# A 512-column matmul for the high and low activations of a dense expert loop, with one subtraction moved to GpSimd

## The chip, the cores and the metric

One core of one Trainium2 chip runs the whole kernel. The metric is device time in microseconds (us); the number to predict is the median over runs of the changed kernel.

## The reference

The kernel computes one decoder layer for 512 tokens of width 1024: a mixing sub-layer (sparse attention beside a gated linear recurrence), a layer norm, a PEER sub-layer with 16384 single-neuron experts, and a second layer norm. Only the PEER part is touched:

```python
q = (xb @ w_q).reshape(PEER_BLOCK, PEER_HEADS, 2, PEER_KEY_DIM // 2)
s = jnp.einsum('thpd,hpkd->thpk', q, sub_keys).astype(jnp.float32)
...
g = jax.nn.softmax(best, axis=-1).astype(xb.dtype)
h = jax.nn.gelu(jnp.einsum('td,thkd->thk', xb, u[experts]))
return jnp.einsum('thk,thkd->td', g * h, v[experts])
```

Every token picks 128 experts (8 heads of 16). Its output is the sum over them of g * gelu(x.u) * v.

## The kernel before

The tokens stand in four blocks of 128. Blocks 0 and 1 take the **row path**: for each of the 128 experts of a token, GpSimd issues a gather of a row of `u` or `v` for the 128 tokens (`gather`, L627), and VectorE works it off with one instruction over 1024 columns (`gu` at L651, which also sums; `hsA<-gv` at L664). The gathered rows stand in a ring of GB = 4 buffers. `pump(n)` puts n such rows at a place of the program.

Blocks 2 and 3 take the **dense path** (`dense`): their 256 tokens meet all 16384 experts, 128 experts in each of 128 steps j. The sparse expert weights are first scattered into a matrix G. Then, in each step:

- `into_hidden(j, n, hp)`, n = 0 and 1: half of the transposed rows of `u` (128x512) is loaded and split by `split` into a high part in fp32r (ScalarE, L760) and the low remainder (VectorE, L762). TensorE sums three products into `hp`: u high times h low (`hTl`), u high times h high (`hTh`), u low times h high. The u part is the stationary operand, h is streamed in 256 columns (L771): 24 matmuls in a step.
- `weigh(j, hp)`: ScalarE takes the gelu of `hp` into `w` (L776), VectorE multiplies by G (L777), ScalarE makes the high part `wh` (L779), VectorE the low part `wl` (L781).
- `out_of_hidden(j, n, wh, wl)`: half of the rows of `v` is loaded and split likewise, and for each of two token blocks three products are summed into `acc` (L791): 12 matmuls of 512 columns in a step. The weights used here are those of one step earlier.

The rings of the loop: 4 buffers for `u`, 3 for `v`, 6 for the split parts, 2 each for `hp`, `wh` and `wl`, one for `w`. The rest of the rows of blocks 0 and 1 is spread over the steps by `pump`. The order of the instructions on each engine is not that of the program text: a scheduler sets it when the kernel is built, and each engine then works its own list strictly in order. SyncE (SP) issues the loads of `u` and `v`.

Of the kernel before, what the change touches and what calls it, by code (L numbers as in the profile page):

```python
# [24 lines left out]
DENSE = (2, 3)  # L25
# buffers of the rings of tiles
HGB = 5
# [6 lines left out]
PJ = 16  # L34
# rows of experts worked off at each such place of the program (sel: one at every second step)
PUMP = {"cw": 4, "qi": 4, "hf": 4, "hq": 4, "hi": 4, "hg": 3, "qa": 2, "hgrn": 1, "att": 4, "mix": 1, "sel": 2,
        "q0": 7, "q1": 0, "q2": 0, "q3": 0}
# rows of block 0's sum that the tensor engine takes: after the queries, and beside the dense weights
PEK1 = 14
PEK2 = 38  # L40
PEPRE = 8
PEG = 60
# tokens of each four whose weights ScalarE multiplies in
GACTS = (3, 4)
# a row of experts at every so manyth group of the dense weights
GPUMP = 3
# the dense step by which all rows are worked off
DLAST = 127
# [3 lines left out]
def tile_decoder_layer(ctx, tc, a, out):  # L52
# [70 lines left out]
    def layer_norm(ys, os_, g, b, nm):  # L123
        """Each y is a tile or a list of its parts along the features."""
        n = len(ys)
        mv = cst.tile([128, n, 2], F32, name="mv" + nm, tag="ln_mv", bufs=2)
        parts = [y if isinstance(y, list) else [y[:, k * 512:(k + 1) * 512] for k in range(2)] for y in ys]
        for i in range(n):
            st = cst.tile([128, 2, 6], F32, name=f"st{nm}_{i}", tag="ln_st", bufs=2)
            for k in range(2):  # L130
                nc.vector.bn_stats(st[:, k, :], parts[i][k])  # L131
            nc.vector.bn_aggr(mv[:, i, :], st)
        ve = cst.tile([128, n], F32, name="ve" + nm, tag="ln_ve", bufs=2)
        nc.vector.tensor_scalar(ve, mv[:, :, 1], EPS, None, op0=ALU.add)
        r = rsqrt(ve, n, nm)
        for i, o in enumerate(os_):
            if isinstance(ys[i], list):
                for k in range(2):
                    sl = slice(k * 512, k * 512 + 512)
                    nc.vector.scalar_tensor_tensor(o[:, sl], parts[i][k], mv[:, i, 0:1], g[:, sl],  # L140
                                                   op0=ALU.subtract, op1=ALU.mult)
            else:
                nc.vector.scalar_tensor_tensor(o, ys[i], mv[:, i, 0:1], g, op0=ALU.subtract, op1=ALU.mult)  # L143
            nc.vector.scalar_tensor_tensor(o, o, r[:, i:i + 1], b, op0=ALU.mult, op1=ALU.add)  # L144
# [24 lines left out]
    hsA = cst.tile([128, 2, 1024], F32, name="hsA")  # L169
    hsB = cst.tile([128, 2, 1024], F32, name="hsB", tag="hsB")  # L170
    hTh = cst.tile([128, 8, 256], F32R, name="hTh")
    hs = [hsA[:, 0, :], hsA[:, 1, :], hsB[:, 0, :], hsB[:, 1, :]]
# [6 lines left out]
    def tok_major(blocks, xT, w, name):  # L179
        """x W for each block, tokens on partitions."""  # L180
        ps_ = [bank(f"{name}{b}") for b in blocks]
# [11 lines left out]
    def feat_major(blocks, xT, w, name):  # L193
        """(x W)^T for all blocks at once, features on partitions: a bank for each 128 features."""
        m = w.shape[-1] // 128
# [22 lines left out]
    def lower_bound():  # L218
# [6 lines left out]

        # lower bound of the forget gate: f = fa + fc * tanh(z / 2)
        fa = pre.tile([128, 512], F32, name="fa")
# [41 lines left out]
    def hgrn(b, pr, mixT):  # L269
# [35 lines left out]
        for par in range(2):  # L305
            ap_ = bank(f"at{b}_{par}", "hg")
            for j in range(4):
# [3 lines left out]
                                    tri[:, None, :].to_broadcast([128, 4, 128]), op=ALU.mult)  # L311
        # the states before each chunk of 32
        S = []
# [86 lines left out]
    def select(b, pr):  # L400
        """What to add to the negated attention scores of the keys that the index doesn't choose."""
        nk = (b + 1) * 128
# [90 lines left out]
    def queries(blocks, hT):  # L493
        """Sub-key scores and, for each of the 16 lists, its 16 best."""
        nt = 128 * len(blocks)
# [53 lines left out]
    def best16(b, g, sv, si, bv, pos):  # L549
        # a pair (a, b) can be among the 16 best only if (a + 1) * (b + 1) <= 16; the places keep the pairs' order  # L550
        s4 = sv[:, g * 4:g * 4 + 4, :].rearrange("p (h z) k -> p h z k", z=2)
# [15 lines left out]
    def routing(b, half, sv, si, bv, pos):  # L567
        """The experts and their weights for four of the block's heads."""
        H = slice(half * 4, half * 4 + 4)
        C = slice(half * 64, half * 64 + 64)  # L570
        # place -> the two ranks
        p2 = pos[:, H, :].rearrange("p h k -> p (h k)")
# [20 lines left out]
        nc.vector.tensor_copy(rbb, t1)  # L593
        # rank -> sub-key
        si4 = si.rearrange("p (h z) k -> p h z k", z=2)
# [18 lines left out]
        if b not in DENSE:  # L614
            nc.vector.scalar_tensor_tensor(idx[b][half], val[1], 128.0, val[0], op0=ALU.mult, op1=ALU.add)
        # softmax over the 16 kept, whose first is their maximum
        g3 = gate[:, b, C].rearrange("p (h k) -> p h k", h=4)
# [27 lines left out]
    def peer_gather(b):  # L645
        """Yields True after each row of experts is worked off, False where it waits for pe_gather."""
        hd = cst.tile([128, 128], F32, name=f"hd{b}", tag="hd")
# [24 lines left out]
    def pe_gather(n, p):  # L672
        """A part of block 0's sum over the rows of v on the tensor engine: diag(weight) @ rows; yields after each."""
        while 0 not in weighted:
# [27 lines left out]
    def dense(den, dps):  # L702
        """Tokens of the DENSE blocks against every expert, with the experts' weights scattered to a dense matrix."""
        nb = len(DENSE)
        T = 128 * nb
        tr = {}
        hTl = consts_loaded["hTl"]
        for i, b in enumerate(DENSE):
# [56 lines left out]
        def into_hidden(j, n, hp):  # L765
            u = den.tile([128, 512], F32, name=f"u{j}_{n}", tag="u", bufs=UB)
            nc.sync.dma_start(u.rearrange("p (k i) -> p k i", k=4), a["ut"][j, :, n * 4:n * 4 + 4, :])
            uh, ul = split(f"u{j}_{n}", u)
            for q, (ut, ht) in enumerate(((uh, hTl), (uh, hTh), (ul, hTh))):
                for k in range(4):  # L770
                    nc.tensor.matmul(hp, ut[:, k * 128:(k + 1) * 128], ht[:, n * 4 + k, :],  # L771
                                     start=(n + q + k == 0), stop=(n == 1 and q == 2 and k == 3))

        def weigh(j, hp):
            w = den.tile([128, T], F32, name=f"w{j}", tag="w")
            nc.scalar.activation(w, hp, AF.Gelu_apprx_tanh)  # L776
            nc.vector.tensor_tensor(w, w, G[:, j, :], op=ALU.mult)  # L777
            wh = den.tile([128, T], F32R, name=f"wh{j}", tag="wh", bufs=2)
            nc.scalar.copy(wh, w)  # L779
            wl = den.tile([128, T], F32R, name=f"wl{j}", tag="wl", bufs=2)  # L780
            nc.vector.tensor_tensor(wl, w, wh.bitcast(F32), op=ALU.subtract)  # L781
            return wh, wl

        def out_of_hidden(j, n, wh, wl):
# [3 lines left out]
            for i in range(nb):  # L788
                sl = slice(i * 128, (i + 1) * 128)
                for q, (wt, vt) in enumerate(((wl, vh), (wh, vh), (wh, vl))):  # L790
                    nc.tensor.matmul(acc[i][n], wt[:, sl], vt, start=(j == 0 and q == 0), stop=(j == 127 and q == 2))  # L791

        def residual():
            ia = gat.tile([128, 128], F32, name="ia", tag="dg", bufs=1)
            nc.scalar.mul(ia, ident, ALPHA)
            for i in range(nb):
                for n in range(2):
                    for c in range(4):
                        for t in (hTl, hTh):
                            nc.tensor.matmul(acc[i][n][:, c * 128:(c + 1) * 128],  # L800
                                             t.bitcast(F32)[:, n * 4 + c, i * 128:(i + 1) * 128], ia,
                                             start=False, stop=False)
# [4 lines left out]
        for j in range(129):  # L807
            if j < 128:
                hp = dps.tile([128, 512], F32, name=f"hp{j}", tag="hp", bufs=2)[:, :T]
                into_hidden(j, 0, hp)  # L810
            want = total * min(j + 1, DLAST) // DLAST
            pump(want - due)
# [5 lines left out]
            if j == DLAST:  # L818
                gb = ln2_consts(1)
                finish(1, gb)  # L820
            if j < 128:
                into_hidden(j, 1, hp)
                ws_new = weigh(j, hp)
            if j:
# [7 lines left out]
    def stage(blocks, xT):  # L832
# [31 lines left out]
        if blocks != [0]:  # L864
            hTl = cst.tile([128, 8, 256], F32R, name="hTl", tag="hsB")
            consts_loaded["hTl"] = hTl
            for k in range(0, 8, 2):
                x = hT[:, k:k + 2, 128:384]
                nc.scalar.copy(hTh[:, k:k + 2, :], x)
                nc.vector.tensor_tensor(hTl[:, k:k + 2, :], x, hTh[:, k:k + 2, :].bitcast(F32), op=ALU.subtract)  # L870
            for _ in pe_gather(PEK1, [bank(f"pv{i}", "hg") for i in range(2)]):
# [57 lines left out]
```

## Time and profile before

| what | value |
|---|---|
| runs | 1651.08, 1656.95, 1659.08 us; median 1656.95 |
| span of the profiled execution, first to last instruction | 1647.0 us |
| TensorE matmul busy | 1456.9 us (88%), 7858 matmuls |
| VectorE busy | 1387.7 us (84%) |
| ScalarE busy | 706.5 us (43%) |
| GpSimd busy | 663.7 us (40%) |
| first matmul of the dense loop / last multiplication by G | 882.0 us / 1630.3 us |

The profile gives the span of its execution, which is 10 us below the median of the runs; what lies outside the span is start and end of the program. Busy shares are means over stages with different limits, so the dense loop has to be read by itself. A matmul's duration in the rows is longer than the time until the next may start, since matmuls overlap: their cost in a row of them is read from start to start. The same holds, in a small way, for VectorE, whose next instruction starts some 0.07 us before the one ahead has ended.

### The profile page before, as it was taken

To read this page: it belongs to the slowest core of one execution; us is meant where nothing else is said; L and a number is where in the kernel's file an instruction comes from. 1 tells how busy PE (TensorE), PEld (TensorE's weight loads), DVE (VectorE), ACT (ScalarE), POOL (GpSimd) and SP (SyncE) were. 2 spreads that over 40 slices of the span, in tenths; PEclk is the share of its full clock that TensorE was granted. 3 is DMA by queue.
4 is the path that set the end of the run, shared out by engine and by line. 5 is a ranking of instruction groups with operands and counts; after the bars stand their busy time and mean duration, and the time that the engine had idled before them with its cause. 6 is when DMAs were issued, how large, how long until landed. Compare 5 with 4: busy or idle time off the path is not lost. (4 is left out here: it accounts for less than half of the span.)

```text
span 1647.0 us, 24505 instructions
## 1 busy us (share of the span) xinstructions
PE 1456.9 (88%) x7858; PEld 1096.3 (67%) x7858; DVE 1387.7 (84%) x3263; ACT 706.5 (43%) x1501; POOL 663.7 (40%) x531
## 2 busy tenths in 40 slices
PE   8889899763577899868998999999999999999996
PEld 4567444542333365425667888888888889989885
DVE  4139899787787669998887899998999899999998
ACT  3312321122233010327996555555555555555553
POOL 0003423456665251135443344443444345534540
PEclk9899899755599999989999999999999999999998
DMA  7377878788887785246677999999999999999995
GB/s 284 122 275 248 280 265 290 245 273 275 262 276 252 264 306 186 84 136 226 220 218 263 327 345 351 355 345 344 343 356 344 336 347 359 365 349 345 354 358 191
DMA packets 166161, 467.89 MB, mean 284 GB/s; under 512 B 18576, under 2 KB 18704, under 8 KB 165904
## 3 DMA queue, kind: packets, MB, share of 16 engines
q0 software_dynamic: 73728, 268.47, 48.0%
q1 hardware_dynamic: 92304, 197.86, 33.2%
q8 instruction: 62, 1.02, 0.2%
q14 instruction: 67, 0.55, 0.1%
HBM read 464.16 MB, written 2.10 MB: 283 GB/s over the span
## 5 line engine op out<-in xcount | busy, mean ns | idle before, releaser
L627 POOL DMA_INDIRECT gv<-in_v_dram,idx x256 | 335.1, 1309 | 420.0 <-DVE hsA L664 268.6
L627 POOL DMA_INDIRECT gu<-in_u_dram,idx x256 | 318.6, 1245 | 458.2 <-DVE gu L651 289.3
L651 DVE SCALAR_TENSOR_TENSOR gu<-gu,hsA 128x1024 f32<-128x1024 f32 x256 | 309.5, 1225 | 52.5 <-DMA gu<-in_u_dram,idx 51.9
L664 DVE SCALAR_TENSOR_TENSOR hsA<-gv,gate,hsA 128x1024 f32<-128x1024 f32 x204 | 261.6, 1282 | 30.0 <-DMA gv<-in_v_dram,idx 26.6
L760 ACT CAST v_0h<-v 128x512 fp32r<-128x512 f32 x128 | 79.7, 622 | 96.7 <-PE acc L791 55.4
L518 PE MATMUL pq<-hT,wpq 128*128 128x128 f32 (+1 forms) x512 | 118.8, 390 | 0.0
L760 ACT CAST v_1h<-v 128x512 fp32r<-128x512 f32 x128 | 79.5, 621 | 88.6 <-DMA v<-in_v_dram 45.7
L762 DVE TENSOR_TENSOR u_0l<-u,u_0h 128x512 fp32r<-128x512 f32 x128 | 88.5, 692 | 32.7 <-ACT u_0h L760 29.9
L760 ACT CAST u_0h<-u 128x512 fp32r<-128x512 f32 x128 | 79.4, 620 | 72.2 <-PE hp L771 40.1
L791 PE MATMUL acc<-v_0h,wl 128*128 128x512 f32 x256 | 101.9, 398 | 2.5 <-DVE wl L781 2.5
L518 PEld LDWEIGHTS pq<-hT,wpq 128*128 128x128 f32 x512 | 80.0, 198 | 32.1 <-issue 1.7
L762 DVE TENSOR_TENSOR v_1l<-v,v_1h 128x512 fp32r<-128x512 f32 x128 | 87.8, 686 | 15.8 <-ACT v_1h L760 13.5
L791 PE MATMUL acc<-v_0h,wh 128*128 128x512 f32 x256 | 101.0, 394 | 0.0
L791 PE MATMUL acc<-v_1h,wl 128*128 128x512 f32 x256 | 99.7, 389 | 0.0
L791 PE MATMUL acc<-v_1h,wh 128*128 128x512 f32 x256 | 99.7, 389 | 0.0
L791 PE MATMUL acc<-v_0l,wh 128*128 128x512 f32 x256 | 99.5, 390 | 0.0
L760 ACT CAST u_1h<-u 128x512 fp32r<-128x512 f32 x128 | 79.4, 621 | 46.4 <-PE acc L791 42.3
L735 DVE TENSOR_TENSOR og<-iota,dtr 128x512 f32<-128x512 f32 x128 | 81.6, 687 | 13.6 <-PE gb L744 11.7
L762 DVE TENSOR_TENSOR u_1l<-u,u_1h 128x512 fp32r<-128x512 f32 x128 | 87.8, 686 | 5.1 <-ACT wh L779 2.7
L762 DVE TENSOR_TENSOR v_0l<-v,v_0h 128x512 fp32r<-128x512 f32 x128 | 88.0, 688 | 3.4 <-ACT v_0h L760 2.1
L682 PE MATMUL pw<-gv,dg 128*128 128x512 f32 x152 | 76.0, 623 | 15.6 <-ACT dg L680 9.1
L771 PE MATMUL hp<-hTl,u_0h 128*128 128x256 f32 x512 | 84.3, 287 | 5.8 <-ACT u_0h L760 5.8
(282 smaller groups left out, 3166.6 us busy)
## 6 DMA issues: line engine op xcount, KB each, us to landing
v<-in_v_dram SPq DMA_DIRECT2D x256, 256.0 KB
u<-in_ut_dram SPq DMA_DIRECT2D x256, 256.0 KB
wpq<-in_w_pq_dram SPq DMA_DIRECT2D x32, 512.0 KB
wo<-in_w_o_dram SPq DMA_DIRECT2D x16, 512.0 KB
hfw<-in_w_hf_dram SPq DMA_DIRECT2D x8, 512.0 KB
hqw<-in_w_hq_dram SPq DMA_DIRECT2D x8, 512.0 KB
hiw<-in_w_hi_dram SPq DMA_DIRECT2D x8, 512.0 KB
qaw<-in_w_qa_dram SPq DMA_DIRECT2D x8, 512.0 KB
```

The lines of the kernel that those rows point to most:

```text
L518: nc.tensor.matmul(qp[:, :nt], w[:, k, :], hT[:, k, :nt], start=(k == 0), stop=(k == 7))
L627: nc.gpsimd.indirect_dma_start(out=t, out_offset=None, in_=table, in_offset=bass.IndirectOffsetOnAxis(ap=idx[b][k // 64][:, k % 64:k % 64 ...
L651: nc.vector.scalar_tensor_tensor(g, g, 1.0, hs[b], op0=ALU.mult, op1=ALU.mult, accum_out=hd[:, k:k + 1]))
L664: nc.vector.scalar_tensor_tensor(hs[b], g, gate[:, b, k:k + 1], hs[b], op0=ALU.mult, op1=ALU.add))
L682: nc.tensor.matmul(p[i], dg, g[:, i * 512:(i + 1) * 512], start=(k == ks[0]), stop=(k == ks[-1]))
L735: nc.vector.tensor_tensor(og[n], iota[:, None, :].to_broadcast([128, 4, 128]), x[n][:, c:c + 4, None].to_broadcast([128, 4, 128]), op=ALU. ...
L760: nc.scalar.copy(h, x)
L762: nc.vector.tensor_tensor(l, x, h.bitcast(F32), op=ALU.subtract)
L771: nc.tensor.matmul(hp, ut[:, k * 128:(k + 1) * 128], ht[:, n * 4 + k, :], start=(n + q + k == 0), stop=(n == 1 and q == 2 and k == 3))
L791: nc.tensor.matmul(acc[i][n], wt[:, sl], vt, start=(j == 0 and q == 0), stop=(j == 127 and q == 2))
```

## The change

Three edits in the dense loop. The h parts stand side by side in one tile `hT2` (token columns 0 to 255 high, 256 to 511 low), so that u high meets both in one 512-column matmul. The first 256 columns of `hp` then hold the high sum (and u low times h high), the last 256 the low sum, and `weigh` adds them: ScalarE copies the low half out of PSUM to `lo`, VectorE adds it to the high half. The subtraction for `wl` goes from VectorE to GpSimd, and `wl` is used last of the three products. Both halves of u are written ahead of v in each step. (Comments that the diff deletes are not shown.)

```diff
-    hsB = cst.tile([128, 2, 1024], F32, name="hsB", tag="hsB")
-    hTh = cst.tile([128, 8, 256], F32R, name="hTh")
+    hsB = cst.tile([128, 4, 1024], F32, name="hsB", tag="hsB")
...
             uh, ul = split(f"u{j}_{n}", u)
-            for q, (ut, ht) in enumerate(((uh, hTl), (uh, hTh), (ul, hTh))):
+            def low():
                 for k in range(4):
-                    nc.tensor.matmul(hp, ut[:, k * 128:(k + 1) * 128], ht[:, n * 4 + k, :],
-                                     start=(n + q + k == 0), stop=(n == 1 and q == 2 and k == 3))
+                    nc.tensor.matmul(hp[:, :T], ul[:, k * 128:(k + 1) * 128], hT2[:, n * 4 + k, 0, :],
+                                     start=False, stop=False)
+            if n:
+                low()
+            for k in range(4):
+                nc.tensor.matmul(hp, uh[:, k * 128:(k + 1) * 128], hT2[:, n * 4 + k, :, :].rearrange("p a t -> p (a t)"),
+                                 start=(n + k == 0), stop=(n == 1 and k == 3))
+            if not n:
+                low()
 
         def weigh(j, hp):
             w = den.tile([128, T], F32, name=f"w{j}", tag="w")
-            nc.scalar.activation(w, hp, AF.Gelu_apprx_tanh)
+            lo = den.tile([128, T], F32, name=f"lo{j}", tag="lo")
+            nc.scalar.copy(lo, hp[:, T:])
+            nc.vector.tensor_tensor(w, hp[:, :T], lo, op=ALU.add)
+            nc.scalar.activation(w, w, AF.Gelu_apprx_tanh)
             nc.vector.tensor_tensor(w, w, G[:, j, :], op=ALU.mult)
...
-            nc.vector.tensor_tensor(wl, w, wh.bitcast(F32), op=ALU.subtract)
+            nc.gpsimd.tensor_tensor(wl, w, wh.bitcast(F32), op=ALU.subtract)
             return wh, wl
...
-                for q, (wt, vt) in enumerate(((wl, vh), (wh, vh), (wh, vl))):
+                for q, (wt, vt) in enumerate(((wh, vh), (wh, vl), (wl, vh))):
...
-                hp = dps.tile([128, 512], F32, name=f"hp{j}", tag="hp", bufs=2)[:, :T]
+                hp = dps.tile([128, 512], F32, name=f"hp{j}", tag="hp", bufs=2)
                 into_hidden(j, 0, hp)
+                into_hidden(j, 1, hp)
+                ws_new = weigh(j, hp)
...
-            if j < 128:
-                into_hidden(j, 1, hp)
-                ws_new = weigh(j, hp)
...
-                nc.scalar.copy(hTh[:, k:k + 2, :], x)
-                nc.vector.tensor_tensor(hTl[:, k:k + 2, :], x, hTh[:, k:k + 2, :].bitcast(F32), op=ALU.subtract)
+                nc.scalar.copy(hT2[:, k:k + 2, 0, :], x)
+                nc.vector.tensor_tensor(hT2[:, k:k + 2, 1, :], x, hT2[:, k:k + 2, 0, :].bitcast(F32), op=ALU.subtract)
```

How the change moves instructions is seen at three places, all near the middle of the last third of the loop (rows of `gv` 71 to 76). First VectorE, one step of the kernel before; the names ending in `l` are the low parts of u and v, `hsA<-gv` is a row product.

```order
L664 SCALAR_TENSOR_TENSOR hsA<-gv_72_13061,gate,hsA 128x1024
L777 TENSOR_TENSOR w_13023<-w_13023,G 128x256
L762 TENSOR_TENSOR v_0l<-v_0_13067,v_0h 128x512
L762 TENSOR_TENSOR u_1l<-u_1_13079,u_1h 128x512
L664 SCALAR_TENSOR_TENSOR hsA<-gv_73_13064,gate,hsA 128x1024
L781 TENSOR_TENSOR wl_13028<-w_13023,wh_13026 128x256
L762 TENSOR_TENSOR v_1l<-v_1_13104,v_1h 128x512
L762 TENSOR_TENSOR u_0l<-u_0_13117,u_0h 128x512
```

The same step of the changed kernel on VectorE:

```order
L784 TENSOR_TENSOR w_12585<-hp_12556,lo_12586 128x256
L786 TENSOR_TENSOR w_12585<-w_12585,G 128x256
L663 SCALAR_TENSOR_TENSOR hsA<-gv_72_12595,gate,hsA 128x1024
L761 TENSOR_TENSOR v_1l<-v_1_12613,v_1h 128x512
L761 TENSOR_TENSOR u_0l<-u_0_12626,u_0h 128x512
L663 SCALAR_TENSOR_TENSOR hsA<-gv_73_12598,gate,hsA 128x1024
L761 TENSOR_TENSOR u_1l<-u_1_12640,u_1h 128x512
L761 TENSOR_TENSOR v_0l<-v_0_12670,v_0h 128x512
```

`wl` is gone from VectorE's list and the addition out of PSUM (L784) has come in ahead of the multiplication; the multiplication is followed by a row product, then by the splits.

Second GpSimd, which in the kernel before issued nothing in the loop but the gathers. In the changed kernel its list reads:

```order
L626 DMA gv_75_12667<-in_v_dram,idx_1_109 128x1024
L790 TENSOR_TENSOR wl_12593<-w_12585,wh_12591 128x256
L626 DMA gv_76_12733<-in_v_dram,idx_1_109 128x1024
L626 DMA gv_77_12736<-in_v_dram,idx_1_109 128x1024
L790 TENSOR_TENSOR wl_12662<-w_12654,wh_12660 128x256
```

One subtraction stands between one or two gathers. The buffer of gather 75 is freed by the row product of `gv` 71 (which stands on VectorE right ahead of the addition shown above), that of 76 by the product of 72.

Third TensorE, in the kernel before, from the last product into one `hp` to the first use of that step's weights (`wl_13102` belongs to `hp_13042`):

```order
L771 MATMUL hp_13042<-hTh,u_1l 128x256 x4
L771 MATMUL hp_13116<-hTl,u_0h 128x256 x4
L771 MATMUL hp_13116<-hTh,u_0h 128x256 x4
L791 MATMUL acc_0_5889<-v_0h,wl_13028 128x512
...
L771 MATMUL hp_13116<-hTh,u_1l 128x256 x4
L791 MATMUL acc_0_5889<-v_0h,wl_13102 128x512
```

And in the changed kernel, `wh_12591` and `wl_12593` belonging to `hp_12556`:

```order
L775 MATMUL hp_12556<-hT_4548,u_1h 128x512 x4
L800 MATMUL acc_0_5888<-v_0h,wh_12522 128x512
...
L775 MATMUL hp_12625<-hT_4548,u_0h 128x512 x4
...
L770 MATMUL hp_12625<-hT_4548,u_0l 128x256 x4
L800 MATMUL acc_0_5888<-v_0h,wh_12591 128x512
...
L770 MATMUL hp_12625<-hT_4548,u_1l 128x256 x4
L775 MATMUL hp_12625<-hT_4548,u_1h 128x512 x4
L800 MATMUL acc_0_5888<-v_0l,wh_12591 128x512
L800 MATMUL acc_0_5888<-v_0h,wl_12593 128x512
```

Between the last matmul into `hp_12556` and the first with `wl_12593` the list has 17 `acc` matmuls, 8 of 512 columns into the next `hp` and 8 of 256. In the kernel before it was 12 and 24.

## Rows read from the trace of the kernel before

**Rows 1.** Busy time by stretch (start:end, length, then busy us of each engine):

```profile
core 0: us, PE busy (x) PEld busy (x) DVE busy (x) ACT busy (x) POOL busy (x), PEclk, DMA share, GB/s
882.00:1000.00 118.00, 115.90 (x742) 105.65 (x743) 105.01 (x199) 61.70 (x116) 50.19 (x37) 0.98 0.94 327
...
1200.00:1300.00 100.00, 97.58 (x614) 87.50 (x613) 90.61 (x142) 53.92 (x105) 40.43 (x32) 1.00 0.98 347
...
1400.00:1500.00 100.00, 99.47 (x633) 89.97 (x632) 94.71 (x138) 53.88 (x106) 48.94 (x33) 1.00 0.97 353
...
sum 718.00, PE 708.98 PEld 639.90 DVE 661.30 ACT 383.92 POOL 326.04; mean PE 101.28 PEld 91.41 DVE 94.47 ACT 54.85 POOL 46.58
```

**Rows 2.** Timeline of TensorE, one step (start us, us, instruction):

```profile
1200.47 0.64 PE L771 MATMUL hp<-hTh,u_1l 128*128 128x256 f32 x4
...
1203.70 0.64 PE L771 MATMUL hp<-hTl,u_0h 128*128 128x256 f32 x4
...
1206.57 0.40 PE L791 MATMUL acc<-v_0h,wl 128*128 128x512 f32 x1
...
1208.64 0.39 PE L791 MATMUL acc<-v_1h,wh 128*128 128x512 f32 x1
```

**Rows 3.** Groups by line, 900 to 1600 us (count | busy, mean ns | idle before):

```profile
L664 DVE SCALAR_TENSOR_TENSOR hsA<-gv,gate,hsA 128x1024 f32<-128x1024 f32 x120 | 153.4, 1278 | 0.1
L651 DVE SCALAR_TENSOR_TENSOR gu<-gu,hsA 128x1024 f32<-128x1024 f32 x101 | 119.9, 1219 | 0.2 <-DMA gu<-in_u_dram,idx 0.2
...
L777 DVE TENSOR_TENSOR w<-w,G 128x256 f32<-128x256 f32 x120 | 50.3, 419 | 2.6 <-ACT w L776 2.6
L781 DVE TENSOR_TENSOR wl<-w,wh 128x256 fp32r<-128x256 f32 x120 | 50.2, 418 | 0.0
L779 ACT CAST wh<-w 128x256 fp32r<-128x256 f32 x120 | 48.4, 403 | 18.0 <-DVE w L777 17.5
L776 ACT ACTIVATE w<-hp 128x256 f32<-128x256 f32 x121 | 46.1, 381 | 25.0 <-PE hp L771 18.8 <-DVE wl L781 5.6
```

**Rows 4.** Timeline of VectorE, one step of 1419 to 1432 us:

```profile
1422.65 1.28 DVE L664 SCALAR_TENSOR_TENSOR hsA<-gv,gate,hsA 128x1024 f32<-128x1024 f32 x1
1423.85 0.42 DVE L777 TENSOR_TENSOR w<-w,G 128x256 f32<-128x256 f32 x1
1424.18 0.68 DVE L762 TENSOR_TENSOR v_0l<-v,v_0h 128x512 fp32r<-128x512 f32 x1
1424.79 1.28 DVE L664 SCALAR_TENSOR_TENSOR hsA<-gv,gate,hsA 128x1024 f32<-128x1024 f32 x1
...
1429.46 0.42 DVE L777 TENSOR_TENSOR w<-w,G 128x256 f32<-128x256 f32 x1
```

**Rows 5.** Line 349, VectorE with one operand in PSUM (min/median/max ns):

```profile
L349 DVE TENSOR_TENSOR o<-o,gs x8: 417/420/425, 58.3 to 432.8; 128x256 f32<-128x256 f32 x8
```

**Rows 6.** Groups of GpSimd outside the loop:

```profile
L265 POOL TENSOR_TENSOR gs<-gs,ghg 128x512 f32<-128x512 f32 x4 | 5.0, 1270 | 54.4 <-DMA wo<-in_w_o_dram 54.4
...
masks.py:197 POOL MEMSET ident<- 128x128 f32 x1 | 0.2, 204 | 0.3 <-POOLq L919 0.3
```

**Rows 7.** Timelines of GpSimd and VectorE near 287 us, GpSimd first:

```profile
287.08 1.26 POOL L265 TENSOR_TENSOR gs<-gs,ghg 128x512 f32<-128x512 f32 x1
...
287.46 1.97 DVE L651 SCALAR_TENSOR_TENSOR gu<-gu,hsA 128x1024 f32<-128x1024 f32 x1
```

**Rows 8.** Timeline of GpSimd: a gather's issue alone, and two in the loop:

```profile
505.53 0.94 POOL L627 DMA_INDIRECT gv<-in_v_dram,idx  x1 [0.87 <-DVE hsA L664]
...
1424.20 1.48 POOL L627 DMA_INDIRECT gv<-in_v_dram,idx  x1 [1.44 <-DVE hsA L664]
1426.34 2.08 POOL L627 DMA_INDIRECT gv<-in_v_dram,idx  x1 [0.65 <-DVE hsA L664]
```

**Rows 9.** Timeline of VectorE, the low part of w that follows rows 2:

```profile
1205.76 0.42 DVE L781 TENSOR_TENSOR wl<-w,wh 128x256 fp32r<-128x256 f32 x1
```

More of the change, by code (lines that the diff above doesn't have):

```diff
@@ L706, in dense @@
         tr = {}
-        hTl = consts_loaded["hTl"]
+        hT2 = consts_loaded["hT2"]
         for i, b in enumerate(DENSE):
@@ L798, in residual @@
                     for c in range(4):
-                        for t in (hTl, hTh):
+                        for t in (1, 0):
                             nc.tensor.matmul(acc[i][n][:, c * 128:(c + 1) * 128],
-                                             t.bitcast(F32)[:, n * 4 + c, i * 128:(i + 1) * 128], ia,
+                                             hT2.bitcast(F32)[:, n * 4 + c, t, i * 128:(i + 1) * 128], ia,
                                              start=False, stop=False)
@@ L864, in stage @@
         if blocks != [0]:
-            hTl = cst.tile([128, 8, 256], F32R, name="hTl", tag="hsB")
-            consts_loaded["hTl"] = hTl
+            hT2 = cst.tile([128, 8, 2, 256], F32R, name="hT2", tag="hsB")
+            consts_loaded["hT2"] = hT2
             for k in range(0, 8, 2):
                 x = hT[:, k:k + 2, 128:384]
-                nc.scalar.copy(hTh[:, k:k + 2, :], x)
-                nc.vector.tensor_tensor(hTl[:, k:k + 2, :], x, hTh[:, k:k + 2, :].bitcast(F32), op=ALU.subtract)
+                nc.scalar.copy(hT2[:, k:k + 2, 0, :], x)
+                nc.vector.tensor_tensor(hT2[:, k:k + 2, 1, :], x, hT2[:, k:k + 2, 0, :].bitcast(F32), op=ALU.subtract)
             for _ in pe_gather(PEK1, [bank(f"pv{i}", "hg") for i in range(2)]):
```

## The prediction, made before the changed kernel had run

> **What bounds the kernel now.** I read the busy time by stretch first [rows 1]. The dense loop, from 882 us to the end, is the only place that the change touches, and there four things are nearly full at once: TensorE shows 97 to 99 us busy in 100, the DMA engines 0.94 to 0.98 of their time, VectorE 90 to 95. The granted clock is 0.98 to 1.00, so TensorE runs at its upper level, 2.4 GHz, all along. GpSimd is busy less than half of the time. Next I asked what one step costs. Between 900 and 1600 us there are 120 multiplications by G [rows 3], so a step takes 700 / 120 = 5.83 us.
>
> TensorE's own need is read from start to start [rows 2]: 24 matmuls of 256 columns from 1203.70 to 1206.57, 2.87 us or 0.120 each; nine of 512 columns from 1206.57 to 1208.64, 0.230 each, so 12 take 2.76. Together that is 5.63 us of the 5.83: TensorE is the nearest bound.
>
> VectorE's need is read in the same way [rows 4]: a row product takes 1.20 us to the next start, a 256-column operation 0.33, a 512-column one 0.61. There are 101 + 120 row products in 120 steps [rows 3], 1.84 a step; I take 1.17 for the mean, since those of `gu` are some 0.06 shorter [rows 3]. A step is 4 x 0.61 + 2 x 0.33 + 1.84 x 1.17 = 5.25 us. So VectorE has 0.58 us of slack in a step, but only on average: in a step with two row products, as the one of rows 4, it needs 5.50 of the 5.61 us from one multiplication by G to the next. It is the second bound, 0.1 us behind the first where rows are dense. The page's chain of waits holds only the last per cents of the span and does not help here.
>
> **The change, part by part.**
>
> *Matmuls.* Out go 16 matmuls of 256 columns in a step, in come 8 of 512: 8 x 0.230 - 16 x 0.120 = -0.08 us, since the number of columns stays and only the gap between two matmuls is saved. TensorE's need falls to 5.55 us. If TensorE alone set the time, this would be worth 128 x 0.08 = 10 us.
>
> *The sum of the halves.* ScalarE gets a 256-column copy out of PSUM, priced as its 256-column gelu out of PSUM, 0.38 us [rows 3]; ScalarE is 54% busy [rows 1] and goes to some 60%, so it is hidden. VectorE gets a 256-column addition with one operand in PSUM. An operation of that very form stands outside the loop with 0.420 us [rows 5], the `wl` that leaves VectorE takes 0.418 [rows 3]. So VectorE's own work does not change: what the move frees, the addition fills.
>
> *The subtraction on GpSimd.* Its price is not in the trace at this size. Two-operand work on GpSimd is there at 512 columns, 1.27 us [rows 6]. Half of that, 0.64, is the lower end, the whole of it the upper one. I take a fixed part of 0.2 us, as the shortest full-height instruction of GpSimd shows [rows 6], and half of the remaining 1.07: 0.74 us. That is work for an engine with room. What counts is what it does to VectorE meanwhile. Near 287 us GpSimd's two-operand instruction runs from 287.08 to 288.34; a row product starts on VectorE at 287.46 and takes 1.97 us where its kind takes 1.22 [rows 7]. It was held for 0.75 us, to 288.21, 0.13 before GpSimd's instruction ended. In the other direction, a gather's issue takes 0.94 us alone and 1.48 or 2.08 in the loop [rows 8]: at 1424.20 it falls into a split on VectorE and ends at 1425.68, 0.82 after that split, so that most of its 0.94 came behind it [rows 4]. So the two engines shut each other out while both read operands from SBUF in pairs. Each `wl` therefore holds VectorE for 0.74 - 0.13 = 0.61 us, unless VectorE would have waited anyway. The order of the instructions says that it would not: behind the multiplication by G stands a row product, and behind that mostly splits, all with two operands in SBUF. The bounds of the hold are 0.5 (from 0.64) and 1.14 (from 1.27); nothing at all is left as a rival below.
>
> The Trainium skill states the same lock more strictly (SBUF — State Buffer, "Who interferes with whom": the second to issue fully blocks until the first finishes). By that the hold would be the whole 0.74 us, and the forecast 128 x 0.13 = 17 us higher; the row of 287 us lets VectorE go 0.13 us before the end, and the sum goes by the row.
>
> *The order.* GpSimd's list puts each `wl` between gathers. A gather waits for the row product that frees its buffer, and the ones ahead of a `wl` are freed by products ahead of that step's addition, so no `wl` waits for something late on VectorE; a gather behind a `wl` is used four row products later, which covers a microsecond. On SP the loads of u and v change places within a step and none is added: nothing there. The old chain from `hp` to `wl` took from 1201.11 (1200.47 + 0.64) to 1206.18 [rows 2, 9], 5.07 us, and its `wl` was used at 1206.57. The new one has a copy and an addition more, but the list leaves it 25 x 0.23 + 8 x 0.12 = 6.7 us up to the first matmul with `wl`, against 12 x 0.23 + 24 x 0.12 = 5.6 before. I cost it at nothing, and keep its failure as a rival.
>
> *Ahead of the loop* the copies into `hT2` are as many as those into `hTh` and `hTl`: nothing.
>
> **The sum.** VectorE's need becomes 5.25 + 0.61 = 5.86 us in a mean step, above TensorE's 5.55 and just above the present 5.83. A pipeline that is bound by VectorE does not run without gaps: in the best step of before 0.11 us were left (5.61 - 5.50), and steps with two row products (6.11 + 0.11) are not fully made up by those with one. I take 0.17 us of gaps: 6.03 us a step, 0.20 more than now, times 128 = **+26 us**. The profiled span becomes 1647 + 26 = 1673 us; the median of the runs stands 10 us above that span for what lies outside it, so 1657 + 26 = **1683 us**.
>
> About 0.5% (8 us) either way is what a measurement of this kernel can tell from no change.
>
> **The rivals.**
>
> *TensorE stays the bound and the change pays.* If the hold falls where VectorE would have waited (0.58 us a step on average), TensorE's saving shows: -0.08 x 128 = -10 us, 1647. If the looser order also takes away part of the 0.20 us that TensorE loses now, the DMA engines come next: at 0.97 busy they need 0.97 x 5.83 = 5.66 us, -22 us, 1635. For it: the average slack is nearly as large as the hold, and `wl` no longer ties VectorE to ScalarE's `wh`. Against it: in the dense steps the slack is 0.1, not 0.58. Chance 0.20.
>
> *The hold is half hidden.* Each step ends between 5.77 and 5.89 us: 1649 to 1665 us. This is also what happens if the move does not do what it says, that is, if the lock shuts out GpSimd alone, until VectorE happens to wait, and the 10 us are lost to late `wl`. Chance 0.20.
>
> *The subtraction is as dear as the 512-column one.* With 1.27 us the hold is 1.14, the step 5.25 + 1.14 + 0.17 = 6.56: +0.73 x 128 = +93 us, 1750. For it: the output is fp32r, which no GpSimd row shows. Against it: most of the 1.27 goes with the columns if the fixed part is 0.2. Chance 0.08.
>
> *TensorE waits for `wl`.* The bare instructions of the chain go from 0.38 + 0.42 + 0.40 + 0.42 = 1.6 to 0.38 + 0.42 + 0.38 + 0.42 + 0.40 + 0.74 = 2.7 us; the old chain spent 5.07 - 1.6 = 3.5 us in queues. With one more wait behind a row product (1.2) the new one takes 7.4 us, 0.7 over the 6.7 that the list allows: +90 us, 1747. It decides once the queues cost more than 4.0 us. Chance 0.09.
>
> **How the numbers follow.** The forecast, VectorE held by GpSimd, has 0.43: with a hold of 0.55 to 0.8 us and gaps of 0.1 to 0.3 it gives 1666 to 1715. Slower by over 0.5% is 0.43 + 0.08 + 0.09 = 0.60, within 0.5% 0.20, faster 0.20. The range reaches from 1640, which leaves out the far part of the first rival, to 1730, which leaves out most of the two dear ones: between them some 0.8 lies.
>
> **What the changed profile would show.** Right: row products or splits on VectorE that begin inside a `wl` last 0.4 to 0.75 us longer than 1.22 or 0.69, about one in each step, so that the mean of one of these groups rises by several tenths of a us; VectorE shows 97% or more in the middle of the loop and TensorE falls to 92 to 94%; the clock stays at 1.00; the DMA share falls to about 0.94; `wl` on GpSimd takes 0.7 us and more with waits. Wrong: those groups keep their means (no hold), or VectorE's share falls below 92 (not the bound), or the matmuls wait for `wl` by tenths of a us in each step (the chain).

## The result, and the profile after

| | before | after |
|---|---|---|
| median of 6 runs each, us | 1654.01 | 1720.46 (1713.92 to 1735.2) |
| ratio after / before, 95% interval | | 1.0412 [1.0371, 1.0453] |
| span of the profiled execution, us | 1647.0 | 1713.6 |
| first to last multiplication by G, us | 739.9 | 806.6 |
| the same, per step | 5.83 | 6.35 |

The changed kernel is slower by 66 us, where 26 were forecast; the time lies inside the range, near its upper end. All of it is in the dense loop: 806.6 - 739.9 = 66.7 us.

Busy time of two stretches of the changed kernel (columns as in [rows 1]):

```profile
core 0: us, PE busy (x) PEld busy (x) DVE busy (x) ACT busy (x) POOL busy (x), PEclk, DMA share, GB/s
1100.00:1200.00 100.00, 90.80 (x431) 72.11 (x430) 89.37 (x151) 52.03 (x109) 53.65 (x43) 0.98 0.89 306
1400.00:1500.00 100.00, 96.51 (x462) 75.94 (x461) 96.93 (x131) 56.15 (x117) 56.49 (x48) 1.00 0.95 334
```

In the later stretch VectorE is as full as the forecast said. In the earlier one nothing is: TensorE stands at 91, VectorE at 89, DMA at 0.89. Where no engine is full, the engines wait for each other or for loads, and there the forecast falls shortest: between 900 and 1200 us a step takes 6.58 us (5.81 before), between 1220 and 1600 us 6.15 (5.77 before), each from multiplication by G to multiplication by G.

The groups of the changed kernel, 900 to 1660 us:

```profile
L663 DVE SCALAR_TENSOR_TENSOR hsA<-gv,gate,hsA 128x1024 f32<-128x1024 f32 x117 | 153.0, 1308 | 0.6 <-ACT hsA L659 0.6
...
L650 DVE SCALAR_TENSOR_TENSOR gu<-gu,hsA 128x1024 f32<-128x1024 f32 x103 | 142.5, 1415 | 0.4 <-DMA gu<-in_u_dram,idx 0.4
L790 POOL TENSOR_TENSOR wl<-w,wh 128x256 fp32r<-128x256 f32 x120 | 139.3, 1161 | 262.9 <-issue 256.2 <-ACT wh L788 6.6
...
L761 DVE TENSOR_TENSOR v_0l<-v,v_0h 128x512 fp32r<-128x512 f32 x120 | 100.3, 836 | 2.8 <-ACT v_0h L759 2.7
...
L800 PE MATMUL acc<-v_0h,wl 128*128 128x512 f32 x239 | 91.5, 394 | 0.8 <-POOL wl L790 0.8
L761 DVE TENSOR_TENSOR v_1l<-v,v_1h 128x512 fp32r<-128x512 f32 x119 | 88.1, 740 | 8.6 <-ACT v_1h L759 8.3
...
L800 PE MATMUL acc<-v_1h,wh 128*128 128x512 f32 x238 | 79.3, 415 | 34.0 <-ACT v_1h L759 33.9
...
L759 ACT CAST v_1h<-v 128x512 fp32r<-128x512 f32 x119 | 73.7, 620 | 99.7 <-DMA v<-in_v_dram 88.1 <-DVE u_0l L761 5.3 <-PE hp L775 4.1
```

Three groups of the kernel before that answer to them and stand in none of the rows ahead, 900 to 1600 us:

```profile
L627 POOL DMA_INDIRECT gv<-in_v_dram,idx x124 | 181.3, 1462 | 206.8 <-DVE hsA L664 197.8 <-DVE gu L651 4.9 <-DVE v_0l L762 3.8
...
L762 DVE TENSOR_TENSOR v_0l<-v,v_0h 128x512 fp32r<-128x512 f32 x120 | 82.6, 688 | 3.2 <-ACT v_0h L760 2.1 <-issue 0.8
...
L760 ACT CAST v_1h<-v 128x512 fp32r<-128x512 f32 x120 | 74.5, 621 | 84.3 <-DMA v<-in_v_dram 44.0 <-PE hp L771 21.3 <-PE acc L791 14.3
```

Two things have changed. The `gu` products went from 1219 ns [rows 3] to 1415, the splits `v_0l` from 688 to 836: work on VectorE that has not changed takes longer. And ScalarE waits 88.1 us for loads of `v` ahead of `v_1h` (44.0 before), with TensorE behind it, 33.9 us for `v_1h` (0.0 before). TensorE waits for `wl` only 0.8 us in all.

The first of the two is the **lock**, as this document calls it when a GpSimd instruction and one of VectorE that both read two operands from SBUF hold each other up. VectorE near 1425 us, then GpSimd at the same time:

```profile
1424.54 1.28 DVE L663 SCALAR_TENSOR_TENSOR hsA<-gv,gate,hsA 128x1024 f32<-128x1024 f32 x1
1425.74 1.22 DVE L761 TENSOR_TENSOR v_0l<-v,v_0h 128x512 fp32r<-128x512 f32 x1
1426.89 1.27 DVE L663 SCALAR_TENSOR_TENSOR hsA<-gv,gate,hsA 128x1024 f32<-128x1024 f32 x1
```

```profile
1425.20 1.22 POOL L790 TENSOR_TENSOR wl<-w,wh 128x256 fp32r<-128x256 f32 x1 [2.48 <-issue]
```

The split takes 1.22 us where its kind takes 0.68, so it was held for 0.54; with its own 0.68 it ran from 1426.28, 0.14 before `wl` ended at 1426.42. `wl` in turn begins under a row product and takes 1.22 us where the fastest took 0.73: each holds the other up.

The second thing is the ring of buffers for `v`. VectorE, SP, ScalarE and TensorE of the changed kernel near 1105 us:

```profile
1104.80 0.68 DVE L761 TENSOR_TENSOR v_0l<-v,v_0h 128x512 fp32r<-128x512 f32 x1
1105.77 0.69 DVE L761 TENSOR_TENSOR v_1l<-v,v_1h 128x512 fp32r<-128x512 f32 x1 [0.28 <-ACT v_1h L759]
```

```profile
1105.51 1.30 SPq L795 DMA_DIRECT2D v<-in_v_dram  x2
```

```profile
1110.59 0.62 ACT L759 CAST v_1h<-v 128x512 fp32r<-128x512 f32 x1 [1.50 <-DMA v<-in_v_dram]
```

```profile
1111.26 0.73 PE L800 MATMUL acc<-v_1h,wh 128*128 128x512 f32 x2 [1.02 <-ACT v_1h L759]
```

With three buffers the load of `v_1` of one step takes the buffer that `v_0` of the step before gives up, when its split `v_0l` is done. Here that is at 1105.48; the load is issued at 1105.51, and ScalarE, idle for 1.50 us, begins `v_1h` 5.08 us later. The page of the changed kernel gives the median load of `v` (the last number, us):

```profile
v<-in_v_dram SPq DMA_DIRECT2D x256, 256.0 KB, 5.3
```

What counts is how long after the end of `v_0l` ScalarE comes to the next `v_1h`. It is 6.35 us in the median before and 5.48 in the changed kernel, but these have waits for the load in them. With a fourth buffer, in kernels described below, ScalarE doesn't wait for `v`, and they show when it would come: 6.46 us after that split in the old order (e9), 5.05 in the new order alone (e7), 4.06 in the changed kernel (e8). Of 127 steps, 6, 80 and 105 leave less than the 5.3 us. By this count a median load is late with three buffers in most steps of the new order and in few of the old one. Loads vary, and the old order has waits too (44.0 us above), so the count gives the direction and not the size.

### The profile page after: what moved, and what is told of

The parts are those of the page before. It is cut to its first block, busy times and chain, and to the rows that moved or that the text cites. A ratio compares the mean times of both kernels' runs of the same rounds, so it can differ in the third digit from the quotient of the medians.

```text
span 1713.6 us, 23139 instructions
## 1 busy us (share of the span) xinstructions
PE 1474.4 (86%) x6834; PEld 1027.9 (60%) x6834; DVE 1447.6 (84%) x3263; ACT 744.1 (43%) x1629; POOL 782.4 (46%) x659
## 5 line engine op out<-in xcount | busy, mean ns | idle before, releaser
L626 POOL DMA_INDIRECT gv<-in_v_dram,idx x256 | 306.0, 1195 | 267.4 <-DVE hsA L663 84.1
L650 DVE SCALAR_TENSOR_TENSOR gu<-gu,hsA 128x1024 f32<-128x1024 f32 x256 | 330.2, 1305 | 48.0 <-DMA gu<-in_u_dram,idx 47.5
L790 POOL TENSOR_TENSOR wl<-w,wh 128x256 fp32r<-128x256 f32 x128 | 150.7, 1177 | 281.3 <-issue 263.5
L775 PE MATMUL hp<-hT,u_0h 128*128 128x512 f32 x512 | 140.4, 396 | 5.5 <-ACT u_0h L759 5.2
L775 PE MATMUL hp<-hT,u_1h 128*128 128x512 f32 x512 | 140.7, 397 | 0.0
L800 PE MATMUL acc<-v_1h,wh 128*128 128x512 f32 x256 | 85.3, 414 | 34.6 <-ACT v_1h L759 34.6
L775 PEld LDWEIGHTS hp<-hT,u_0h 128*128 128x128 f32 x512 | 93.3, 188 | 34.1 <-ACT u_0h L759 15.8
L761 DVE TENSOR_TENSOR v_0l<-v,v_0h 128x512 fp32r<-128x512 f32 x128 | 106.8, 834 | 2.8 <-ACT v_0h L759 2.7
L800 PE MATMUL acc<-v_1l,wh 128*128 128x512 f32 x256 | 101.2, 396 | 2.3 <-DVE v_1l L761 1.9
L775 PEld LDWEIGHTS hp<-hT,u_1h 128*128 128x128 f32 x512 | 88.8, 191 | 11.6
```

The lines of the kernel that those rows point to most:

```text
L626: nc.gpsimd.indirect_dma_start(out=t, out_offset=None, in_=table, in_offset=bass.IndirectOffsetOnAxis(ap=idx[b][k // 64][:, k % 64:k % 64 ...
L650: nc.vector.scalar_tensor_tensor(g, g, 1.0, hs[b], op0=ALU.mult, op1=ALU.mult, accum_out=hd[:, k:k + 1]))
L761: nc.vector.tensor_tensor(l, x, h.bitcast(F32), op=ALU.subtract)
L775: nc.tensor.matmul(hp, uh[:, k * 128:(k + 1) * 128], hT2[:, n * 4 + k, :, :].rearrange("p a t -> p (a t)"), start=(n + k == 0), stop=(n == ...
L790: nc.gpsimd.tensor_tensor(wl, w, wh.bitcast(F32), op=ALU.subtract)
```

## The experiments

Two causes were on the table, and a third as a rival. **The lock**: `wl` on GpSimd holds VectorE. **The order**: with u ahead of v, `v_1h` comes sooner after the `v_0l` of the step before, and the ring of three makes its load late. **The chain**: the longer way from `hp` to `wl` (copy, addition, slower subtraction) makes TensorE wait. The first four kernels take the change apart.

**e1: the changed kernel, with the subtraction back on VectorE.**

```diff
-            nc.gpsimd.tensor_tensor(wl, w, wh.bitcast(F32), op=ALU.subtract)
+            nc.vector.tensor_tensor(wl, w, wh.bitcast(F32), op=ALU.subtract)
```

> The changed kernel with the wl subtraction back on VectorE; merge and order stay. Theory 1 (lock): GpSimd's subtraction holds one two-operand instruction of VectorE for 0.55 us in each step and that is all of the loss; then this kernel stands within 8 us of the kernel before, v_0l is back at 0.69 us, and waits of ScalarE for loads of v fall from 88 us to the 65 of before. Theory 2 (order): u ahead of v lets the second load of v go out late, and that is all of the loss; then it stays 55 to 70 us above the kernel before with the same waits for v (80 to 90 us). Theory 3 (both, about half each): 25 to 40 us above.

1688.88 against 1660.01, 1.0185 [1.013, 1.0239]. More than half of the loss goes with the subtraction's place on GpSimd, but not all: something else in the change costs 1.8%.

**e2: the changed kernel, with the second half of u back behind the first half of v.**

```diff
                 into_hidden(j, 0, hp)
-                into_hidden(j, 1, hp)
-                ws_new = weigh(j, hp)
...
+            if j < 128:
+                into_hidden(j, 1, hp)
+                ws_new = weigh(j, hp)
```

> The changed kernel with the products of the second half of u, and weigh, back behind the first half of v; merge and GpSimd subtraction stay. Theory 1 (lock): 55 to 70 us above the kernel before; some instruction of VectorE is still 0.55 us longer in each step. Theory 2 (order): within 8 us of the kernel before, waits of ScalarE for v at 65 us or less. Theory 3 (both): 25 to 40 us above.

1758.69, 1.0585 [1.0542, 1.0628]: 99 us above, outside all that was expected. Without the new order the rest is dearer still: the order costs something and saves something.

**e3: the kernel before, with the subtraction alone on GpSimd** (the edit of e1, backwards).

> The kernel before with nothing changed but the engine of the wl subtraction. Theory 1 (lock): 45 to 70 us slower than the kernel before, although VectorE loses 0.34 us of work in each step (in the changed kernel the addition fills that), so 15 to 30 us if the freed 44 us are made use of. Theory 2 (order): no slower, 0 to 20 us faster. Theory 3: 0 to 25 us slower.

1731.73, 1.0425 [1.0384, 1.0466], 72 us above. Groups of e3, 900 to 1600 us:

```profile
L781 POOL TENSOR_TENSOR wl<-w,wh 128x256 fp32r<-128x256 f32 x109 | 120.1, 1102 | 52.6 <-ACT wh L779 50.9
L762 DVE TENSOR_TENSOR v_1l<-v,v_1h 128x512 fp32r<-128x512 f32 x109 | 101.3, 930 | 19.0 <-ACT v_1h L760 18.5
L791 PE MATMUL acc<-v_0h,wl 128*128 128x512 f32 x218 | 95.3, 437 | 49.4 <-POOL wl L781 48.3
```

The lock is there (`v_1l` 930 ns, 686 before), and here the chain is too: TensorE waits 48.3 us for `wl`, since this kernel uses it first of the three products. In e2, which also has the old order but uses `wl` last, TensorE doesn't wait for it in that stretch. So e3 cannot price the lock alone.

**e4: the kernel before, with the new order alone.**

```diff
                 into_hidden(j, 0, hp)
+                into_hidden(j, 1, hp)
+                ws_new = weigh(j, hp)
...
-            if j < 128:
-                into_hidden(j, 1, hp)
-                ws_new = weigh(j, hp)
```

> The kernel before with nothing changed but the place in the program of the second half of u and weigh. Theory 1 (lock): within 8 us of the kernel before. Theory 2 (order): 50 to 70 us slower, ScalarE waits for v for 80 us or more. Theory 3 (both): 20 to 40 us slower.

1685.4, 1.016 [1.0097, 1.0224]. Nothing is computed elsewhere, no matmul has changed, and 1.6% is lost. ScalarE's group of e4, 900 to 1600 us:

```profile
L760 ACT CAST v_1h<-v 128x512 fp32r<-128x512 f32 x116 | 71.9, 620 | 142.6 <-DMA v<-in_v_dram 117.7 <-DVE u_0l L762 15.8 <-PE hp L771 4.7
```

117.7 us of waits for `v` against 44.0 before. The order costs by itself.

**e5 and e6: is it the lock?** e5 adds to the kernel before a subtraction on GpSimd whose result nobody reads; the lists of the other engines stay as they were. e6 adds two writes of zeros into `w` instead, behind its last use: work for GpSimd that reads nothing. The two take 0.64 us together, somewhat less than the 0.73 of an unhindered subtraction, and not longer as was expected.

```diff
+            jk = den.tile([128, T], F32, name=f"jk{j}", tag="jk")
+            nc.gpsimd.tensor_tensor(jk, w, wh.bitcast(F32), op=ALU.subtract)
             return wh, wl
```

> The kernel before with one more subtraction in each step, on GpSimd, of the same form (256 columns, w less wh), into a tile that nobody reads; wl stays on VectorE, and VectorE's, TensorE's and ScalarE's lists are those of the kernel before, instruction by instruction. Lock: one two-operand instruction of VectorE is longer by about 0.55 us in each step, 60 to 70 us of VectorE in all, of which its idle time takes a part: 15 to 45 us slower. If the lock is not the price of the move, but a late wl that TensorE waits for: within 8 us of the kernel before, since nobody waits for this result.

```diff
+            for _ in range(2):
+                nc.gpsimd.memset(w, 0.0)
             return wh, wl
```

> The kernel before with two memsets of 256 columns over w on GpSimd behind each step's wl: GpSimd is busy for longer than with a subtraction, the next gelu waits for it in the same way, but it reads nothing from SBUF. Lock on the shared reading of operands: VectorE's instructions keep their durations and the kernel is within 8 us of the kernel before. If any work on GpSimd costs as much (late gathers, a busy queue): 15 to 45 us slower, as with the subtraction.

e5 takes 1707.15 against 1650.86, 1.0334 [1.0295, 1.0372]; e6 takes 1650.71, 0.9991 [0.9969, 1.0013]. Groups of e5, then of e6, 900 to 1600 us:

```profile
L783 POOL TENSOR_TENSOR jk<-w,wh 128x256 f32<-128x256 f32 x111 | 137.3, 1237 | 44.0 <-ACT wh L779 42.2
...
L762 DVE TENSOR_TENSOR u_0l<-u,u_0h 128x512 fp32r<-128x512 f32 x112 | 94.8, 847 | 10.5 <-ACT u_0h L760 8.1 <-PE acc L793 1.3
L762 DVE TENSOR_TENSOR v_1l<-v,v_1h 128x512 fp32r<-128x512 f32 x111 | 94.5, 851 | 4.3 <-ACT v_1h L760 2.2 <-PE hp L771 1.0 <-issue 0.9
...
L781 DVE TENSOR_TENSOR wl<-w,wh 128x256 fp32r<-128x256 f32 x112 | 62.7, 560 | 0.0
...
L776 ACT ACTIVATE w<-hp 128x256 f32<-128x256 f32 x112 | 43.0, 384 | 103.1 <-POOL jk L783 48.2 <-PE hp L771 39.0 <-DVE wl L781 14.7
```

```profile
L762 DVE TENSOR_TENSOR u_0l<-u,u_0h 128x512 fp32r<-128x512 f32 x120 | 82.9, 691 | 22.6 <-ACT u_0h L760 20.0 <-issue 0.2
L762 DVE TENSOR_TENSOR v_1l<-v,v_1h 128x512 fp32r<-128x512 f32 x120 | 82.2, 685 | 12.7 <-ACT v_1h L760 9.5 <-PE hp L771 2.6
...
L783 POOL MEMSET w<- 128x256 f32 x240 | 76.2, 318 | 34.1 <-DVE wl L781 26.2 <-DVE rs_tl L119 0.9
...
L776 ACT ACTIVATE w<-hp 128x256 f32<-128x256 f32 x120 | 46.1, 384 | 80.2 <-POOL w L783 60.3 <-PE hp L771 16.8 <-PE acc L793 2.3
```

In e5 the splits rise to 847 and 851 ns, and VectorE's own `wl` from 418 [rows 3] to 560; in e6 they keep their 691 and 685. Both kernels make the next gelu wait for GpSimd, since there is one `w` (48.2 us and 60.3 us), so that wait is not the price: e6 has more of it and loses nothing. What costs is a GpSimd instruction that reads two operands beside VectorE, and nobody reads its result. Whether one operand would be enough was not tried. The loss, 56 us, is above the 15 to 45 that were expected: the hold is 0.71 us in a step here, and nothing has left VectorE.

**e7: the new order with a fourth `v` buffer.** Room for it comes from `wl`, which moves into tiles that are dead by then; the same edit (below) serves e8 to e11.

```diff
-VB = 3
+VB = 4
...
-                keep[b] = [cst.tile([128, 128], F32, name=f"ij{b}_{z}", tag="ij", bufs=4) for z in range(2)]
+                ij = cst.tile([128, 256], F32, name=f"ij{b}", tag="ij", bufs=2)
+                keep[b] = [ij[:, z * 128:(z + 1) * 128] for z in range(2)]
...
-            wl = den.tile([128, T], F32R, name=f"wl{j}", tag="wl", bufs=2)
+            wl = cst.tile([128, T], F32R, name=f"wl{j}", tag="ij", bufs=2)
```

> The kernel before with only the order changed (it was 25 us slower), and a fourth buffer for v; its room comes from wl, which goes into the tiles of the expert numbers that are dead by then. If the order costs because v_1's load waits for the buffer that v_0 of the step before frees: ScalarE's waits for loads of v fall from 118 to below 30 us and the kernel comes within 8 us of the kernel before, or below it. If the order costs by the list itself (weigh early, v late): 15 to 25 us slower still.

1650.29, 0.9997 [0.9978, 1.0016]: the 1.6% of e4 is gone, and so are the waits. ScalarE's group of e7, 900 to 1600 us, where loads of `v` stand no longer among the releasers:

```profile
L761 ACT CAST v_1h<-v 128x512 fp32r<-128x512 f32 x120 | 74.3, 619 | 55.5 <-PE hp L772 29.7 <-PE acc L792 19.7 <-DVE gu L652 1.6
```

In e4 and e7 the scheduler also set different lists, so that more than the buffer differs. e10 below settles this: it is e1 with a fourth buffer, and from 882 us on all engines have e1's list but for two neighbours on VectorE that change places once.

**e8: the changed kernel with a fourth `v` buffer**, which leaves the lock and takes the ring away.

> The changed kernel with a fourth buffer for v. If the two costs add (25 us from the ring, about 32 from the lock, 4 from the merge): 30 to 45 us above the kernel before. If late loads are only what the lock makes of them: still 55 to 65 us above.

1679.01, 1.0172 [1.0134, 1.0211], 28 us above, a little less than the 30 to 45 expected. Busy time of e8 in the last part, then a group, 900 to 1660 us:

```profile
1400.00:1600.00 200.00, 194.60 (x937) 155.46 (x936) 194.33 (x262) 112.79 (x233) 121.59 (x96) 1.00 0.96 337
```

```profile
L762 DVE TENSOR_TENSOR v_0l<-v,v_0h 128x512 fp32r<-128x512 f32 x126 | 105.4, 837 | 2.2 <-ACT v_0h L760 2.1
```

VectorE is 97% busy, the splits are as long as in the changed kernel, and from the first to the last multiplication by G it takes 764.5 us, 6.02 a step: the 6.03 of the forecast. e10 below differs from e8 only in the engine of the subtraction and takes 741.0 us, e7 takes 736.4. So the changed kernel's 67 us are 764.5 - 741.0 = 24 for the lock, 741.0 - 736.4 = 5 for the merge (which the runs' medians cannot tell from nothing) and 806.6 - 764.5 = 42 for the ring, less the 3.5 that e7's loop is shorter than that of before. The costs don't simply add: the ring costs 764.5 - 736.4 = 28 us with the order alone (e4 against e7) and 42 here. That the lock makes the ring dearer by delaying the very split that frees the buffer fits the row at 1425.74, but was not tried by itself; the lists of e8 and of the changed kernel differ too.

**e9: the kernel before with a fourth `v` buffer**, to see whether the buffer helps it too.

> The kernel before with a fourth buffer for v and no other change: the control of the two runs with that buffer. If the ring of v holds up only the new order: within 8 us of the kernel before. If it holds up the old order too (ScalarE waited 65 us for loads of v there): 10 to 20 us faster, down to what the DMA engines allow.

1665.33 against 1656.44, 1.0047 [1.0024, 1.0069]: it does not; it is 9 us slower, a little more than the 8 expected as the most. Why is open; the lists of VectorE and ScalarE differ here too. The fourth buffer repairs what the new order breaks and is worth nothing by itself.

**e10: the merge and the order with a fourth buffer, the subtraction on VectorE** (e1 and the edit of e7).

> The changed kernel without the lock (wl on VectorE) and without the late loads (four buffers for v): what is left is the merge of the matmuls in the new order. If the merge saves what the matmuls' starts say: 5 to 10 us faster than the kernel before. If its longer chain (copy, addition) gives that back, as the 4 us between the runs with and without the merge at three buffers say: within 8 us.

1661.61 against 1656.44, 1.0019 [0.9994, 1.0043]. ScalarE's group of `v_1h`, 900 to 1600 us, of e1 and then of e10:

```profile
L759 ACT CAST v_1h<-v 128x512 fp32r<-128x512 f32 x115 | 71.4, 621 | 91.5 <-DMA v<-in_v_dram 73.5 <-PE hp L770 8.1 <-PE acc L800 4.5
```

```profile
L760 ACT CAST v_1h<-v 128x512 fp32r<-128x512 f32 x119 | 74.0, 621 | 18.3 <-PE acc L801 12.7 <-PE hp L776 3.9 <-ACT w L786 0.4
```

With the same lists the fourth buffer takes away 73.5 us of waits for `v`, and the loop falls from 772.7 to 741.0 us. That shows the ring as the cause, at 32 us, with nothing else changed. Beside e7's 0.9997 the merge brings nothing that can be measured. Busy time of e10 in the last part, then the gathers of `gv`, 900 to 1600 us:

```profile
1400.00:1600.00 200.00, 200.00 (x988) 160.51 (x987) 198.56 (x311) 122.68 (x246) 150.21 (x65) 1.00 0.99 358
```

```profile
L627 POOL DMA_INDIRECT gv<-in_v_dram,idx x115 | 260.6, 2266 | 95.7 <-DVE hsA L664 85.5 <-DVE gu L651 5.7 <-DVE u_1l L762 3.3
```

TensorE, VectorE (99%) and the DMA engines (0.99) are all full: shorter matmuls leave the same work to the other two. But e10 does not price the shorter matmuls alone: with the subtraction back on VectorE, the merge's addition comes on top of it there, 0.33 us or more in each step.

**e11: as e10, in the old order.**

> As the run before, but with the old order: merge alone, wl on VectorE, four buffers for v. If the chain from hp to wl decides, the old order leaves it less time and this one is 10 to 40 us slower than the kernel before; if not, it stands within 8 us of the run before.

1727.3, 1.0425 [1.0389, 1.046], 71 us above, where 40 were the most expected. Waits of e11, 900 to 1600 us (waiter, releaser: us in all, times, longest us):

```profile
ACT wh L789 <- DVE w L787: 61.3, 92, 1.2
DVE u_0l L762 <- ACT u_0h L760: 54.8, 91, 1.2
...
PE hp L771 <- DVE u_1l L762: 35.4, 51, 1.1
```

In the old order the merge costs 4%. The waits run from VectorE over ScalarE back to VectorE and on to TensorE: with the copy and the addition `weigh` has four hand-overs between the two engines up to `wh`, where it had two, and in that list u's splits stand behind them. That is how the waits read; no run takes them apart. With u ahead of v the same merge takes 1.0019 (e10), so the new order does save this; with three buffers it pays for it in late loads.

All kernels together; "order" is u ahead of v, "wl" the engine of the subtraction; the kernels with the merge also use `wl` last of the three products:

| kernel | merge | order | wl | v buffers | ratio |
|---|---|---|---|---|---|
| before | no | old | VectorE | 3 | 1 |
| e9 | no | old | VectorE | 4 | 1.0047 |
| e3 | no | old | GpSimd | 3 | 1.0425 |
| e4 | no | new | VectorE | 3 | 1.016 |
| e7 | no | new | VectorE | 4 | 0.9997 |
| e1 | yes | new | VectorE | 3 | 1.0185 |
| e10 | yes | new | VectorE | 4 | 1.0019 |
| e11 | yes | old | VectorE | 4 | 1.0425 |
| e2 | yes | old | GpSimd | 3 | 1.0585 |
| after | yes | new | GpSimd | 3 | 1.0412 |
| e8 | yes | new | GpSimd | 4 | 1.0172 |

None is faster than the kernel before.

## Why the prediction was right in its direction and short in its size

**The subtraction on GpSimd: right, the hold a little smaller.** Alone it took 0.732 us at its fastest (0.74 forecast). The 0.2 us taken as its fixed part came from a row that isn't the shortest of GpSimd (memsets of one column, 128 partitions high, took 0.10 us in the kernel before); with 0.1 the estimate would have been 0.69, so that it met this well is in part luck. The hold was 0.54 us in the row above, and 0.54 in the median of the 119 instructions of VectorE that were held in the loop (0.61 forecast); together that is 62 us, 0.48 for each `wl`. In the mean `v_0l` and `gu` are 148 and 196 ns longer, since a `wl` meets now one and now another. VectorE came free 0.14 us before GpSimd's end (0.13 forecast). The rule of the Trainium skill (SBUF — State Buffer, "Who interferes with whom") has the direction right, and the row here shows again that VectorE doesn't wait for the whole instruction. All lines of the changed kernel together:

```profile
L790 POOL TENSOR_TENSOR wl<-w,wh x128: 732/1162/3007, 889.6 to 1695.9; 128x256 fp32r<-128x256 f32 x128
```

```profile
L784 DVE TENSOR_TENSOR w<-hp,lo x128: 406/411/426, 886.4 to 1692.8; 128x256 f32<-128x256 f32 x128
```

The addition took 0.411 us (0.42 forecast). That its longest took 0.426 says nothing on the lock: it writes the one `w` that the `wl` before it reads, so it never ran beside a `wl`.

**The sum over VectorE: right once the ring is out of the way, but in part by luck.** e8 shows 6.02 us a step and 28 us in all, where 6.03 and 26 were forecast. The hold in it is 0.48 us a step where 0.61 were forecast; the rest, VectorE's own work and its gaps, is 6.02 - 0.48 = 5.54 where 5.25 + 0.17 = 5.42 were. The two misses cancel. A slip stands in the forecast's own bounds: a hold of 0.8 and gaps of 0.3 make 6.35 us a step, and that gives 1724 us, not 1715.

**The order: this is the step that failed.** "On SP the loads of u and v change places within a step and none is added: nothing there." The count was right and the conclusion wrong. What had to be asked is when each load may start, and when its data are wanted: a buffer of `v` comes free with a split on VectorE, and the new order brings ScalarE to the next `v_1h` about 1.4 us sooner after that split: 5.05 us in e7, which is less than a load takes, 6.46 in e9, which is more. The kernel before already waited 44.0 us for that load ahead of `v_1h`, in a view that the prediction does not use. A term that was put at nothing is 28 us with the order alone (e4 against e7), 32 with the merge (e1 against e10) and 42 beside the lock. None of the rivals was this one: that the measured time lies inside the range is luck, since the upper part of the range stood there for a dearer subtraction and a late `wl`.

**The matmuls: the size of the term was right, and no gain showed.** In the changed kernel matmuls of 512 columns into `hp` start 0.229 us apart in the median and those of 256 0.120, as forecast. The forecast gave -0.08 us only "if TensorE alone set the time". With the lock and the ring removed (e10 against e7) VectorE, which has the addition besides, and the DMA engines are full, and nothing shows.

**The chain: right for the change, for the reason given.** 0.8 us of waits for `wl`, which is used last. Used first, in the old order, it makes TensorE wait 48.3 us (e3); used last in the old order, not at all (e2).

**The time outside the span: wrong, without weight.** The 10 us put outside the span were mostly the difference between runs: the changed kernel's profiled run took 1715.4 us, 1.8 more than its span.

**What the profile was to show.** Between 1400 and 1500 us VectorE reached 96.9% (97 forecast) and the DMA share fell to 0.95 (0.94 forecast); TensorE fell to 96.5, not to 92 to 94. Between 1100 and 1200 us VectorE stayed under the 92 that the prediction had named as the sign that it was not the bound. That sign was true: there VectorE was not the bound, and the loads of `v` were late.

## What to carry to other kernels

Work that reads two operands from SBUF is not free on GpSimd while VectorE does the same: here each such instruction of 0.73 us took 0.48 from VectorE in the mean and relieved it of 0.42. When a change moves consumers in time, work out for each ring of buffers how long it is from the release of a buffer to its next use, and set it against the time a load takes to land, even if no load is added; a distance measured with waits in it looks longer than it is, and waits for that load that are in the profile already say how near the edge it is. And in a loop where three resources are over 90% full, do not count on the saving of one before the others have room.

## What the runs showed of the hardware that had not been expected

The issue of a gather on GpSimd, 0.94 us alone [rows 8], took 1.46 us in the mean for `gv` in the kernel before, with VectorE at 90 to 95% [rows 1], and 2.27 in e10 with VectorE at 99%. The gathers of `gu` did not follow (1.40 before, 1.37 in e10), so VectorE's busy share alone does not decide it; what does is open. In the other direction nothing is seen, so that the prediction's "the two engines shut each other out" holds for the subtraction and not for a gather: beside the gather of 1424.20 the row product of 1424.79 took its usual 1.28 us [rows 4, 8], and in the kernel before, between 900 and 1600 us, the longest of 120 such products took 1.285. Writes of zeros (0.318 us each, e6) neither lengthened the splits of VectorE, of which most `u_0l` and `v_1l` ran beside one, nor cost time; this had been expected when e6 was put on record. Whether an instruction of VectorE with one operand in PSUM is held stays open, since none ran beside a `wl`.
